# A hybrid encoder layer on one core: a written order with a fixed map of SBUF and PSUM, eight gate tiles moved into block products, and latent attention in quarter tiles

## The chip, the cores and the metric

The kernel runs on one core of a Trainium2 chip. The metric is the device time of one execution in microseconds (us). The core's engines work side by side and meet at semaphores: PE (TensorE, matmuls), DVE (VectorE), ACT (ScalarE), POOL (GpSimd), and SP (SyncE), which here only issues DMAs. PE writes to PSUM, which has eight banks of 128 partitions x 512 float32.

## The reference

One layer on 1024 tokens of 1024 channels, in float32. A single projection of the normed input feeds two attentions and their gates:

```python
h = rmsnorm(x, attn_norm_g)
(c_q, c_kv, k_rope, z_mla, q_dil, k_dil, v_dil, z_dil, g_mla, g_dil) = split(h @ w_in)
a_out = mla_attention(c_q, c_kv, k_rope, ...)       # 8 heads, dense, queries and keys of 64 + 32
y_mla = (a_out * silu(z_mla)) @ w_o_mla
d_out = dilated_mixture(q_dil, k_dil, v_dil, ...)   # 3 groups of 8 heads of 64:
                                                    # (window, dilation) = (128,1), (512,4), (2048,16)
y_dil = (d_out * silu(z_dil)) @ w_o_dil
merged = sigmoid(g_mla + b) * y_mla + sigmoid(g_dil + b) * y_dil
out = rmsnorm(x + merged @ w_out, final_norm_g)
```

The three groups of the dilated mixture are combined by the softmax of their log denominators, so after a pair of heads is done in all three groups, its results are multiplied by factors made from all three.

## The kernel before, in words

Every float32 operand of a product is split into a high part (a cast on ACT, type fp32r) and a low part (a subtraction on DVE or POOL), and a product is three matmuls, high x high, low x high and high x low. That is `mm3` (L77 to L79), and `split` (L83, L84) makes the parts. A **step** below is one such triple with 512 columns.

The work goes in stages. (1) Latents and the values of the dilated groups, up to 221 us. (2) **Block products** up to 452 us: the q and k channels of the dilated groups, in pairs of 128-channel tiles, each pair as a 2 x 2 block matrix product with seven products instead of eight. One product is 4 x 3 = 12 matmuls of 512 columns. Sums of the products on ACT and DVE (`block_steps`, L464), operands and differences on POOL (`block_operand`, `block_minus`), five products ahead. The results go to DRAM (`s_dq`, `s_dk`), and come back in the form that attention wants (`op_b`, `op_a`). (3) **Dilated attention** up to about 800 us: four pairs of heads, three groups in each pair, a unit at a time: scores of two blocks (`s_ps`, L861, L862, and L973 for the widest group), maxima and masks on DVE (L871), exponentials on ACT (L878), transposes on PE (`pt`, L885), their split (ACT L893, DVE L897), values (`av`, L909, L916, L1004), and the result, for which ACT copies one half (`av_t`, L921) and DVE adds the other (`num`, L935). After a pair comes the combine: denominators go through DRAM (`s_sd`, `c_sn`), factors are made from them, go through DRAM too (`s_rr`) and come back spread over partitions (`bc`), where DVE (L1134) and POOL multiply with them. (4) **Latent attention** up to 1142 us: scores of 128 x 1024 (`s_mla`, two banks), maxima (`m_nm`, L741), exponentials (L744), transposes (L755), splits (L83, L84), values (L763, L764). (5) **Output** to the end: what is left of the output projections of both branches (`pj`), the merge with the gates (`gate`, L1183, L1184), and `w_out` with the last norm.

Stages 3 and 4 are pipelines over DVE and ACT in which PE would wait, so PE is given **fillers** between their pieces: first the steps of the 24 tiles of `z` and merge gates (16 steps each; tile results `zg_z`, `zg_t` go to DRAM as `s_zs`, `s_gt`), then the output projections of the dilated branch, then those of the latent branch, as far as they are ready. `feed(n)` gives out n steps on the average; `FIRST_FEED` steps go ahead of the first scores, and `DIL_FEED` and `FEED` are the rates.

What sets the order: in stage 3 the program order is kept on each engine (a manual schedule). In stage 4 and 5 the tile framework's scheduler places instructions, fillers anchored behind a matmul (`issue_after`). Space in SBUF and PSUM is from pools that open and close by stage; a tile that reuses space waits for what used it. In stage 3 the eight banks are two for `pt`, two for `pj`, two tiles of one bank each for `s_ps`, and two of one bank each for `av`. In stage 4 they are two for `pt`, one for `pj`, one for `av`, and two tiles of two banks for `s_mla`. Loads and stores all go through SP's queue in program order, each waiting there for its data.

## Time and profile before

| what | value |
|---|---|
| median of three runs | 1271.56 us (1269.66 to 1273.31) |
| profiled execution, its own time | 1270.74 us |
| span of its trace | 1269.0 us |
| mean granted clock of PE | 0.991 |
| PE busy | 1227.3 us, 97% |
| DVE, ACT, POOL busy | 59%, 48%, 40% |
| chain that ended last: PE, DMA, DVE | 71%, 12%, 5% |
| PE busy, 447 to 473 us (start of dilated attention) | 22.62 of 26 us |
| PE busy, 473 to 800 us (dilated attention) | 317.30 of 327 us |
| PE busy, 800 to 1134 us (latent attention) | 331.42 of 334 us |
| PE busy, 1134 to 1176 us (start of output) | 34.21 of 42 us |
| PE busy, 1176 us to the end | 86.67 of 93 us |

The rows quoted from the trace have a start time, a duration, the engine, the line of the program, the operation, the tiles out<-in, the shape, and in brackets the engine's idle time just before, with what ended it. Starts of matmuls are measured, their ends modelled, so the pace of PE is read from start to start. A row of the waits view names what waited, for what, the total, how often, and the longest. Lines of the kernel before are those of its own listing above; the change has other line numbers.

### The profile page before, as it was taken

To read this page: it belongs to the slowest core of one execution; us is meant where nothing else is said; L and a number is where in the kernel's file an instruction comes from. 1 tells how busy PE (TensorE), PEld (TensorE's weight loads), DVE (VectorE), ACT (ScalarE), POOL (GpSimd) and SP (SyncE) were. 2 spreads that over 40 slices of the span, in tenths; PEclk is the share of its full clock that TensorE was granted. 3 is DMA by queue.
4 is the path that set the end of the run, shared out by engine and by line. 5 is a ranking of instruction groups with operands and counts; after the bars stand their busy time and mean duration, and the time that the engine had idled before them with its cause. 6 is when DMAs were issued, how large, how long until landed. Compare 5 with 4: busy or idle time off the path is not lost.

```text
span 1269.0 us, 19689 instructions
## 1 busy us (share of the span) xinstructions
PE 1227.3 (97%) x6957; PEld 1071.7 (84%) x6957; DVE 750.3 (59%) x1368; ACT 608.1 (48%) x1276; POOL 506.5 (40%) x402
## 2 busy tenths in 40 slices
PE   8999999999999989998999999999999999997998
PEld 8988999788888878887988888888888888885786
DVE  7473525566666645576566664655656666668632
ACT  6633346344434436655555652455555545554422
POOL 2361219887777624526231132312212212237522
PEclk9999999999999999999999999999999999999999
DMA  9957684267456486878889796455336534135441
GB/s 321 273 162 274 220 290 143 92 183 176 125 137 171 128 229 186 212 192 227 210 210 239 185 242 170 152 133 142 113 104 183 134 101 145 59 108 183 165 150 50
DMA packets 134482, 219.43 MB, mean 173 GB/s; under 512 B 37160, under 2 KB 66672, under 8 KB 130480
## 3 DMA queue, kind: packets, MB, share of 16 engines
q1 hardware_dynamic: 134384, 218.17, 59.7%
q8 instruction: 55, 0.90, 0.3%
q14 instruction: 43, 0.35, 0.1%
HBM read 149.37 MB, written 68.75 MB: 172 GB/s over the span
## 4 chain that ended last, share of the span: by engine, by line
PE 71%; DMA 12%; DVE 5%; issue 4%; SPq 3%; POOL 3%; ACT 2%; DVEq 0%; ACTq 0%; POOLq 0%
PE pj L77 12%; PE pj L79 11%; PE pj L78 11%; PE pt L755 4%; SPq L73 3%; PE av L764 2%; PE av L763 2%; DMA bc<-s_rr 2%; PE s_mla L77 2%; PE s_mla L79 2%; PE s_mla L78 2%; PE st_c L77 2%; PE st_c L79 2%; PE st_c L78 2%; PE st_d L77 2%
## 5 line engine op out<-in xcount | busy, mean ns | idle before, releaser
L84 POOL TENSOR_TENSOR w_l<-w_raw,w_h 128x512 fp32r<-128x512 f32 (+1 forms) x176 | 227.6, 1306 | 409.4 <-ACT w_h L83 351.2
L77 PE MATMUL pj<-hT_h,w_h 128*128 128x512 f32 x384 | 157.4, 410 | 0.0
L78 PE MATMUL pj<-hT_l,w_h 128*128 128x512 f32 x384 | 151.7, 395 | 0.0
L79 PE MATMUL pj<-hT_h,w_l 128*128 128x512 f32 x384 | 151.7, 395 | 0.0
L83 ACT CAST w_h<-w_raw 128x512 fp32r<-128x512 f32 (+1 forms) x176 | 104.2, 615 | 89.5 <-POOL w_raw L428 77.6
L84 DVE TENSOR_TENSOR pt_l<-pt,pt_h 128x512 fp32r<-128x512 f32 x128 | 87.9, 688 | 65.7 <-ACT pt_h L83 64.9
L83 ACT CAST pt_h<-pt 128x512 fp32r<-128x512 f32 x128 | 74.5, 584 | 80.8 <-PE pt L755 49.1
L77 PE MATMUL pj<-w_h,hT_h 128*128 128x256 f32 x384 | 109.6, 285 | 0.0
L79 PE MATMUL pj<-w_h,hT_l 128*128 128x256 f32 x384 | 109.5, 285 | 0.0
L78 PE MATMUL pj<-w_l,hT_h 128*128 128x256 f32 x384 | 109.4, 285 | 0.0
L741 DVE TENSOR_REDUCE m_nm<-s_mla 128x1 f32<-128x1024 f32 x64 | 78.1, 1221 | 27.8 <-PE s_mla L79 27.3
L871 DVE CUSTOM_DVE_ANT_0 p<-s_ps,masks 128x256 f32<-128x256 f32 x128 | 48.9, 419 | 66.5 <-PE s_ps L862 57.9
L878 ACT ACTIVATE p<-p,d_st 128x256 f32<-128x256 f32 x128 | 64.1, 502 | 48.3 <-DVE d_st L871 48.0
L79 PEld LDWEIGHTS pj<-hT_h,w_l 128*128 128x128 f32 x384 | 73.0, 190 | 16.3
L77 PEld LDWEIGHTS pj<-hT_h,w_h 128*128 128x128 f32 x384 | 73.6, 192 | 11.1
L78 PEld LDWEIGHTS pj<-hT_l,w_h 128*128 128x128 f32 x384 | 73.7, 192 | 10.9
L744 ACT ACTIVATE p<-s_mla,m_nm 128x1024 f32<-128x1024 f32 x64 | 71.8, 1122 | 17.6 <-PE pt L755 16.8
L755 PE MATMUL pt<-consts,p 128*128 128x128 f32 x512 | 78.0, 272 | 1.6 <-ACT p L744 1.5
L77 PEld LDWEIGHTS pj<-w_h,hT_h 128*128 128x128 f32 x384 | 74.2, 193 | 0.9
L78 PEld LDWEIGHTS pj<-w_l,hT_h 128*128 128x128 f32 x384 | 74.1, 193 | 0.8
L79 PEld LDWEIGHTS pj<-w_h,hT_l 128*128 128x128 f32 x384 | 74.2, 193 | 0.7
L763 PE MATMUL av<-pt_h,op_c 128*128 128x256 f32 x256 | 68.6, 288 | 0.0
(306 smaller groups left out, 3303.3 us busy)
## 6 DMA issues: line engine op xcount, KB each, us to landing
w_raw<-wt SPq DMA_DIRECT2D x48, 512.0 KB, 3.7
op_b<-s_dq SPq DMA_DIRECT2D x32, 512.0 KB, 7.4
gate<-s_gt SPq DMA_DIRECT2D x43, 256.0 KB, 2.9
s_dq<-dq_st SPq DMA_DIRECT2D x80, 128.0 KB, 2.4
s_dk<-dq_st SPq DMA_DIRECT2D x80, 128.0 KB, 2.4
s_dv<-dv_st SPq DMA_DIRECT2D x32, 256.0 KB, 4.6
s_gt<-zg_t SPq DMA_DIRECT2D x32, 256.0 KB, 3.3
w_raw<-wv SPq DMA_DIRECT2D x12, 512.0 KB, 3.8
```

What stands on the lines that cost most here:

```text
L73: self.nc.sync.dma_start(out=out, in_=in_)
L77: mm(out, lh, rh, start=start, stop=False, skip_group_check=skip)
L78: mm(out, lh, rl, start=False, stop=False, skip_group_check=skip)
L79: return mm(out, ll, rh, start=False, stop=stop, skip_group_check=skip)
L83: self.nc.scalar.copy(out=h, in_=raw)
L84: sub.tensor_tensor(out=l, in0=raw, in1=h.bitcast(F32), op=ALU.subtract)
L741: v.tensor_reduce(out=nm[:, hh, qb:qb + 1], in_=s, axis=AX.X, op=ALU.max, negate=True)
L744: nc.scalar.activation(out=p, in_=s, func=AF.Exp, bias=nm[:, hh, qb:qb + 1], accum_out=den[:, hh, qb:qb + 1])
L755: self.anchor = nc.tensor.transpose(pt[:, o:o + 128], P[b2][:, 128 * kc:128 * kc + 128], self.ident)
L763: nc.tensor.matmul(a_out, vv[:, kc], ph[:, s], start=kc == 0, stop=False)
L871: nc.vector.tensor_tensor_reduce(out=p[:, c], in0=x["s"][:, c], in1=mask, op0=ALU.add, op1=ALU.min, scale=-0.125, scalar=3e38, accum_out=s ...
L878: nc.scalar.activation(out=p, in_=p, func=AF.Exp, scale=-1.0, bias=nm, accum_out=den)
```

## The change

Five things change together.

1. **Gate tiles as blocks.** The tiles 8 to 15 (gates of the latent branch), eight of the 24 filler tiles, become four more pairs of block products behind the twelve of q and k. Their sums are multiplied by the row factor (DVE), go through tanh (ACT) and to DRAM (`s_gt`). The fillers of the gate fill fall from 24 to 16 tiles.
2. **One order.** From the end of the block products to the end of the program everything is issued in an order that the program writes out, in a manual schedule.
3. **One map.** SBUF is addressed by fixed offsets in rings (`rings`, `hand`, `get`) from two areas. PSUM has four tiles of one bank (`bank0` to `bank3`) and two tiles of two banks (`bank4`, `bank6`); the rings of `s_ps` and `av2` take the halves of the last two, and `s_mla` the whole of them. In latent attention `pj` keeps one bank, and in the output it takes a ring over the single banks and the halves.
4. **Latent attention in ticks.** A tile of 128 queries x 2 is 4 ticks; in a tick go the transposes of a quarter of the keys, their low, a half of the scores of the next tile, the values of the quarter before, and `feed`. The first ticks overlap the last combine.
5. **Other settings.** Four fillers instead of 19 ahead of the first scores; weights of the output are split earlier, and the last fill steps are kept for the second half of the merge.

```diff
-FIRST_FEED = 19
+FIRST_FEED = 4
 DIL_FEED = (1.43, 1.43, 2.5, 2)
-FEED = (0.95, 0.95)
-NB_S, NB_PT, NB_AV = 2, 2, 1
-ZG = (4, 5, 6, 7, 0, 1, 2, 3, *range(16, 24), *range(8, 16))
+ZG = (4, 5, 6, 7, 0, 1, 2, 3, *range(16, 24))
+BLOCK_GATES = (8, 10, 12, 14)
...
+        self.places.update(pt=b[0:2], pj=b[2:4], s_ps=b[4:6], av2=b[6:8], s_mla=self.wide, m_av=b[3:4])
...
+    def get(self, name, shape=(128, 512), dtype=F32):
+        places = self.places[name]
+        x = places[self.turn[name] % len(places)]
+        self.turn[name] += 1
+        return self.shaped(x, shape, dtype) if isinstance(x, int) else x
...
+                def times():
+                    v.tensor_tensor(out=x, in0=x, in1=self.R[:, c], op=ALU.mult)
+                def tanh():
+                    act.activation(out=t, in_=x, func=AF.Tanh, scale=0.5, bias=self.hb[:, j:j + 1])
+                    self.dma(self.gt[j][:, c], t)
...
+    def mla_tick(self, k, c):
+        self.mla_transposes(k, c)
+        if c == 0:
+            self.mla_low(k, c)
+            self.mla_scores(k + 1, 0)
+            self.mla_values(k - 1, 3)
...
+        elif c == 1:
+            self.mla_exponentials(k + 1, 0)
+            self.mla_low(k, c)
+            self.mla_scores(k + 1, 1)
+            self.mla_values(k, 0)
...
+        else:
+            if c == 2:
+                self.mla_exponentials(k + 1, 1)
+            self.mla_low(k, c)
+            self.feed(self.rate)
+            self.mla_values(k, c - 1)
...
+            if t == 24:
+                run_all(self.fill)
+                self.fill = self.proj_fill()
+                self.owed = 0.0
+            self.rate = 1.8 if t < 24 else 1.55 if t < 112 else 3.0
...
+        self.places["pj"] = [self.banks[i] for i in (2, 4, 5, 6, 7)]
...
+        self.places["pj"] = [self.banks[i] for i in (3, 0, 1, 2, 4, 5, 6, 7)]
...
-                    self.blocks([(T_QK + (g * 2 + quad) * 4 + which * 2, g, quad, which) for quad in range(2) for g in range(3) for which in range(2)], tp, pp)
+                    self.blocks([(T_QK + (g * 2 + quad) * 4 + which * 2, g, quad, which) for quad in range(2) for g in range(3) for which in range(2)] + [(T_ZM + i,) for i in BLOCK_GATES], tp, pp)
+            b = [pp.tile([128, 512], F32, name=f"bank{i}") for i in range(4)]
+            self.wide = [pp.tile([128, S], F32, name=f"bank{i}") for i in (4, 6)]
+            self.banks = b + [x[:, 512 * i:512 * i + 512] for x in self.wide for i in range(2)]
```

How it moves instructions, at three places. First SP's queue at the end of the block products. `s_dq` and `s_dk` are stores of q and k, `op_b` and `op_a` the first loads of attention; in the change `s_gt` are the gate stores, `at5632_2048_r` is the first place of `op_b` and `at22016_1152_r` that of `op_a`. Before:

```order
L73 DMA s_dq2_64<-dq_st10_4651 32x1024 [waits DMAHW3_49,Activation_49]
L73 DMA s_dq2_64<-dq_st10_4651 32x1024 [waits DMAHW4_49]
L73 DMA s_dq2_64<-dq_st10_4651 32x1024 [waits DMAHW5_49]
L73 DMA s_dq2_64<-dq_st10_4651 32x1024 [waits DMAHW6_49]
L73 DMA op_b_4805<-s_dq0_62 64x2048 [waits DMAHW7_49,PE_49]
L73 DMA op_b_4805<-s_dq0_62 64x2048 [waits DMAHW0_49]
L73 DMA op_a_4806<-s_dk0_65 64x1152 [waits DMAHW1_49,PE_49]
L73 DMA op_a_4806<-s_dk0_65 64x1152 [waits DMAHW2_49]
```

and in the change:

```order
L119 DMA s_gt_72<-dq_st00_5363 128x512 [waits DMAHW3_49,Activation_49]
L119 DMA s_gt_72<-dq_st11_5367 128x512 [waits DMAHW4_49,Activation_49]
L119 DMA s_gt_72<-dq_st10_5371 128x512 [waits DMAHW5_49,Activation_49]
L119 DMA s_gt_72<-dq_st01_5376 128x512 [waits DMAHW6_49,Activation_49]
L119 DMA at5632_2048_r_5489<-s_dq0_62 64x2048 [waits DMAHW7_49,Pool_49]
L119 DMA at5632_2048_r_5489<-s_dq0_62 64x2048 [waits DMAHW0_49]
L119 DMA at22016_1152_r_5490<-s_dk0_65 64x1152 [waits DMAHW1_49,Pool_49]
L119 DMA at22016_1152_r_5490<-s_dk0_65 64x1152 [waits DMAHW2_49]
```

The first loads now stand behind four gate stores, each of which waits for an activation of the last gate tiles.

Second, PE in the dilated attention, at a unit of the middle group. Before (`s_ps` and `av2` have a new tile number at each use; `Activation` and `DVE` in the brackets are the counters waited for):

```order
L916 MATMUL av2_5353<-pt_h_5302,op_c_5142 128x256 [waits Activation_49]
L916 MATMUL av2_5353<-pt_l_5303,op_c_5142 128x256 [waits DVE_49]
L916 MATMUL av2_5353<-pt_h_5302,op_c_5142 128x256
L916 MATMUL av2_5353<-pt_l_5303,op_c_5142 128x256
L885 MATMUL pt_5391<-consts_84,p_5310 128x128 [waits PE_49,Activation_49]
L885 MATMUL pt_5391<-consts_84,p_5310 128x128 [waits Activation_49]
L885 MATMUL pt_5391<-consts_84,p_5310 128x128 x2
L861 MATMUL s_ps_5399<-op_a_5160,op_b_5159 128x256
L862 MATMUL s_ps_5399<-op_a_5160,op_b_5159 128x256
```

and in the change, where `bank1` is a `pt`, `bank2` a filler, and every score tile is `bank4_5397` and every value tile `bank6_5398`:

```order
L1056 MATMUL bank1_5394<-consts_84,at97792_512_f_5524 128x128 x2
L1032 MATMUL bank4_5397<-at22016_1152_r_5490,at5632_2048_r_5489 128x256 [waits DVE_49]
L1033 MATMUL bank4_5397<-at22016_1152_r_5490,at5632_2048_r_5489 128x256
L1032 MATMUL bank4_5397<-at22016_1152_r_5490,at5632_2048_r_5489 128x256
L1033 MATMUL bank4_5397<-at22016_1152_r_5490,at5632_2048_r_5489 128x256
L123 MATMUL bank2_5395<-at138752_8192_r_102,w_h_5683 128x512
L124 MATMUL bank2_5395<-at171520_8192_r_103,w_h_5683 128x512
L125 MATMUL bank2_5395<-at138752_8192_r_102,w_l_5684 128x512
L123 MATMUL bank2_5395<-at138752_8192_r_102,w_h_5687 128x512
L124 MATMUL bank2_5395<-at171520_8192_r_103,w_h_5687 128x512
L125 MATMUL bank2_5395<-at138752_8192_r_102,w_l_5688 128x512 [waits Pool_49]
```

Score tiles that alternated between two tiles without a wait of their own now share one tile, and the scores wait for DVE; the same holds for `bank6_5398`, the values.

Third, PE in the latent attention of the change, at a place where one output projection ends and the next begins (`bank2` is the only `pj` bank, `bank3` the values, `bank0` and `bank1` the transposes):

```order
L123 MATMUL bank2_5395<-at122368_1024_r_5429,w_h_9092 128x512
L124 MATMUL bank2_5395<-at134656_1024_r_5430,w_h_9092 128x512
L125 MATMUL bank2_5395<-at122368_1024_r_5429,w_l_9093 128x512
L846 MATMUL bank3_5396<-at60928_512_r_5860,at38400_1024_r_8193 128x256 [waits Activation_49]
L847 MATMUL bank3_5396<-at65024_512_r_5861,at38400_1024_r_8193 128x256 [waits DVE_49]
L846 MATMUL bank3_5396<-at60928_512_r_5860,at38400_1024_r_8193 128x256
L847 MATMUL bank3_5396<-at65024_512_r_5861,at38400_1024_r_8193 128x256
L822 MATMUL bank1_5394<-consts_84,at85504_1024_f_8325 128x128
L822 MATMUL bank1_5394<-consts_84,at89600_1024_f_8344 128x128
L822 MATMUL bank1_5394<-consts_84,at85504_1024_f_8325 128x128
L822 MATMUL bank1_5394<-consts_84,at89600_1024_f_8344 128x128
L123 MATMUL bank2_5395<-at97792_1024_r_5423,w_h_9521 128x512 [waits DVE_49]
```

The first matmul of the new projection waits for DVE to have read the bank, with four values and four transposes between.

More of the change, by code (lines that the diff above doesn't have):

```diff
@@ new lines, in mla_values @@
+    def mla_values(self, k, c):
+        if k < 0:
+            return
+        mm = self.nc.tensor.matmul
+        h, u = self.units[k]
+        if u % 2 == 0 and c == 0:
+            self.av = self.get("m_av")
+        out = self.av[:, 256 * (u % 2):256 * (u % 2) + 256]
+        vv = self.heads[h][2]
+        _, ph, pl = self.pt.pop((k, c))
+        for c2 in range(2):
+            kc = 2 * c + c2
+            x = slice(c2 * 256, c2 * 256 + 256)
+            mm(out, vv[:, kc], ph[:, x], start=kc == 0, stop=False)
+            mm(out, vv[:, kc], pl[:, x], start=False, stop=kc == 7)
@@ new lines, in output, with merge @@
+        mh, ml = {}, {}
+        low = lambda first, n: self.shaped(first, [128, n], F32R)
+        for dt in range(8):
+            mh[dt, 0] = low(49152 + 2048 * dt if dt < 6 else 88064 + 2048 * (dt - 6), 512)
+            ml[dt, 0] = low(32768 + 2048 * dt, 512)
+            mh[dt, 1] = self.hand(RIGHT + 36864 + 4096 * dt, 512, F32R)
+            ml[dt, 1] = low(71680 + 2048 * dt, 512)
+        def merge(dt, half):
+            self.split(self.m1[dt, half], mh[dt, half], ml[dt, half], v)
+        rows = [self.hand(RIGHT + 4096 + 4096 * i, S) for i in range(8)]
@@ new lines, in output @@
+        while self.jobs_done < 24:
+            next(self.fill)
+        for i in range(8):
+            if i < 7:
+                self.wout_load(i + 1, 1)
+            next(self.fill)
+            merge(i, 0)
+            next(self.fill)
+            next(self.fill)
+            self.wout_split(1, nc.gpsimd)
+            while self.jobs_done < 25 + i:
+                next(self.fill)
+        self.dma(gf, a["g_final"].partition_broadcast(128))
+        for t in range(4):
+            first(t)
@@ L1336, in _layout @@
+            self.fill = self.gate_fill()
+            with tc.manual_schedule():
+                self.open_areas()
+                first = len(nc.cur_bb.bb.instructions)
+                self.attention()
+                self.output()
+                self.order_areas(first)
 def _layout(inputs):
```

779 lines of the change are left out of this document (425 added, 354 removed).

## The prediction, made before the changed kernel was run

> **What bounds the kernel now.** I read the page first, then the PE waits stage by stage, then windows and timelines at each wait.
>
> ```profile
> span 1269.0 us, 19689 instructions
> PE 1227.3 (97%) x6957; PEld 1071.7 (84%) x6957; DVE 750.3 (59%) x1368; ACT 608.1 (48%) x1276; POOL 506.5 (40%) x402
> PE 71%; DMA 12%; DVE 5%; issue 4%; SPq 3%; POOL 3%; ACT 2%; DVEq 0%; ACTq 0%; POOLq 0%
> ```
>
> TensorE (PE) is busy for 97%, so its matmuls and its stalls set the time. The waits of PE after the block products, stage by stage (total, times, longest):
>
> ```profile
> PE pt L885 <- ACT p L878: 3.9, 1, 3.9
> PE av L916 <- DVE pt_l L897: 8.4, 5, 3.7
> PE pt L755 <- ACT p L744: 1.5, 1, 1.5
> PE pj L77 <- DVE gate L1183: 4.5, 4, 2.2
> PE pj L77 <- ACT wout_h L83: 2.0, 1, 2.0
> PE pj L77 <- ACT w_h L83: 1.2, 1, 1.2
> ```
>
> Together 21.5 us. After the larger gaps the clock is down: in the windows the column behind POOL is the granted clock.
>
> ```profile
> 473.00:478.00 5.00, 4.48 (x15) 3.70 (x16) 2.92 (x12) 4.64 (x16) 4.50 (x4) 0.50 0.50 157
> 594.00:598.00 4.00, 4.00 (x16) 3.35 (x15) 2.96 (x11) 3.40 (x10) 1.11 (x1) 0.57 0.94 296
> 1161.00:1165.00 4.00, 3.88 (x9) 2.69 (x10) 3.11 (x5) 2.05 (x4) 3.50 (x3) 0.57 0.70 231
> ```
>
> The first costs 5 x 0.50 = 2.5 us, the others 4 x 0.43 = 1.7 us each. The base of the sum is the profiled execution's own 1270.7 us, which is 0.8 us below the median of the runs.
>
> **Fewer matmuls.** Eight gate tiles cost 8 x 2 halves x 8 steps x 3 = 384 matmuls now; as four pairs of block products 4 x 7 x 4 x 3 = 336. All have 512 columns, and these start 0.23 us apart:
>
> ```profile
> 451.46 0.39 PE L77 MATMUL st_d<-hT_h,w_h 128*128 128x512 f32 x1
> 451.69 0.39 PE L78 MATMUL st_d<-hT_l,w_h 128*128 128x512 f32 x1
> ```
>
> 48 x 0.227 = **-10.9 us**, sure from the count. A block pair gives POOL 7 lows and 4 differences of 1.3 us against 7 x 12 x 0.227 = 19 us of PE, so POOL's 14 us stay hidden. The price is elsewhere: steps that fill waits fall from 384 to 256, since the tiles gone were fillers.
>
> ```profile
> L84 POOL TENSOR_TENSOR w_l<-w_raw,w_h 128x512 fp32r<-128x512 f32 (+1 forms) x176 | 227.6, 1306 | 409.4 <-ACT w_h L83 351.2
> ```
>
> **Start of the dilated attention.** Now the loads of the first unit are issued while block products still run (these end at 452.1), and 19 fillers cover the landing:
>
> ```profile
> 446.37 1.14 SPq L73 DMA_DIRECT2D op_b<-s_dq  x2
> 447.60 1.18 SPq L73 DMA_DIRECT2D op_a<-s_dk  x2
> DMA to landing us min/median/max: 8.4/11.6/14.8
> 469.24 0.39 PE L79 MATMUL pj<-hT_h,w_l 128*128 128x512 f32 x1
> 473.52 0.97 PE L885 MATMUL pt<-consts,p 128*128 128x128 f32 x3 [3.89 <-ACT p L878]
> ```
>
> From the first issue to the last landing of the four are about 10.2 us (the second op_a is issued at 448.2 and takes 8.4). In the change four gate stores stand ahead of them on SP, and the last can't go before add, product (DVE) and tanh (ACT) of the last tile:
>
> ```profile
> L84 DVE TENSOR_TENSOR pt_l<-pt,pt_h 128x512 fp32r<-128x512 f32 x128 | 87.9, 688 | 65.7 <-ACT pt_h L83 64.9
> 516.72 0.63 ACT L620 ACTIVATE zg_t<-zg_z 128x512 f32<-128x512 f32 x1 [0.25 <-DVE zg_z L618]
> ```
>
> 2 x 0.69 + 0.63 = 2.0 us after the last product; landing is 12.2 us after it; four fillers are 4 x 0.68 = 2.7 us. PE idles 9.5 us and then pays the slow clock (2.5), 12.0 against today's 3.9 + 2.5 = 6.4: **+5.6 us**. If with less traffic the loads take 8 us it is +3.4; if they are as slow as the median of 11.6, +8.8.
>
> **Shared halves: steady units.** Today a score tile and a value tile have a bank each, two in turn. In the change both live as halves of one two-bank tile, and PE's rows wait for a DVE counter at every reuse of either half: the values of a unit wait until DVE has taken the result of the unit just before, and scores wait for the maxima just before. Whether today's result would be late is seen by laying the two timelines side by side:
>
> ```profile
> 516.56 0.28 PE L916 MATMUL av<-pt_h,op_c 128*128 128x256 f32 x1
> 516.60 1.09 DVE L935 TENSOR_TENSOR num<-av,av_t 64x512 f32<-64x512 f32 x1
> 532.28 0.28 PE L916 MATMUL av<-pt_h,op_c 128*128 128x256 f32 x1
> 532.40 1.09 DVE L935 TENSOR_TENSOR num<-av,av_t 64x512 f32<-64x512 f32 x1
> ```
>
> The result ends at 517.69 where the next values start at 516.56, and at 533.49 where they start at 532.28: late by 1.1 and 1.2 us. Laid out over the whole stage, 13 of the 40 value tiles are late in this way outside the combines, by 0.1 to 1.9 us, 12.5 us in all; the tiles of the first, narrow group never are. PE is in order, and what follows on DVE waits for PE's next scores, so a wait is not made up later. I take **+12.5 us**; low 4 (DVE comes to the result sooner because it is less behind after each wait), high 16.
>
> **Shared halves: combines.** After each pair DVE multiplies by factors that come back by DMA, and stands in its queue until they land:
>
> ```profile
> DVE num L1134 <- DMA bc<-s_rr: 27.3, 12, 5.3
> 580.84 0.69 DVE L1134 TENSOR_TENSOR num<-num,bc 128x512 f32<-128x512 f32 x1 [5.28 <-DMA bc<-s_rr]
> 590.59 1.44 DVE L1134 TENSOR_TENSOR num<-num,bc 128x512 f32<-128x512 f32 x1 [2.74 <-DMA bc<-s_rr]
> 582.36 0.28 PE L916 MATMUL av<-pt_h,op_c 128*128 128x256 f32 x1
> 583.76 0.39 PE L916 MATMUL av<-pt_l,op_c 128*128 128x256 f32 x1 [1.12 <-DVE pt_l L897]
> 590.61 0.28 PE L916 MATMUL av<-pt_h,op_c 128*128 128x256 f32 x1
> 593.38 0.39 PE L916 MATMUL av<-pt_l,op_c 128*128 128x256 f32 x1 [2.49 <-DVE pt_l L897]
> DVE num L1134 <- DMA bc<-s_rr: 4.0, 3, 2.6
> ```
>
> DVE stands 27.3 us, PE only 8.4: PE runs a score tile, fillers and a value tile ahead. The maxima and results queued behind that wait are what PE now asks for one tile sooner. The last row is the last pair alone, 4.0 us (with pieces at the window's edge 5); of the other 22, in seven waits, a slack of about one filler and a half (1 us) remains each: 15 us of stall, against 8.4, and two results late besides (3 us): **+9.5 us**. The low end is 0, if the factors land earlier; the high end 22 - 8.4 + three slow clocks of 1.7 = +19.
>
> **Latent attention.** A pair's tile now takes four ticks. The merge projections that fill it use one PSUM bank, as before, but two steps are given out together, so that a job's end and the next job's start can stand a few matmuls apart, with the DVE read of the bank between. On DVE the low of a split is ahead, and that waits for ACT's cast:
>
> ```profile
> L83 ACT CAST pt_h<-pt 128x512 fp32r<-128x512 f32 x128 | 74.5, 584 | 80.8 <-PE pt L755 49.1
> L675 DVE SCALAR_TENSOR_TENSOR m<-gate,pj 128x512 f32<-128x512 f32 x16 | 10.9, 679 | 4.6 <-PE pj L79 4.6
> 583.98 0.28 PE L916 MATMUL av<-pt_h,op_c 128*128 128x256 f32 x1
> 584.10 0.28 PE L916 MATMUL av<-pt_l,op_c 128*128 128x256 f32 x1
> 584.22 0.60 PE L885 MATMUL pt<-consts,p 128*128 128x128 f32 x4
> 584.57 0.37 PE L861 MATMUL s_ps<-op_a,op_b 128*128 128x256 f32 x1
> ```
>
> 0.58 + 0.69 + 0.68 = 1.95 us on DVE's side, against four values (0.48) and four transposes (0.35) on PE's: 1.1 us each. The order has ten such places (where values and transposes don't stand between, more): **+10 us** with about 1 us each, 4 to 15. Besides, the gate fill ends in the fourth of 32 tiles and the next fill begins three tiles later, and the last combine, covered today by fillers, runs into these ticks: its 5 us, and a little for bare tiles, **+5.5 us** (0 to 12).
>
> **Output.** The six-row list above has 7.7 us of waits here, and 1.7 of slow clock; eleven fill steps kept for this place and the weights split earlier remove most. But the ring of banks contains both halves of the same two tiles, so a part waits for DVE and ACT to leave the neighbour: 4 x 1.4 us (0.69 and 0.63 again). 5.6 - 9.4 = **-4 us** (-9 to +5).
>
> Sum: -10.9 + 5.6 + 12.5 + 9.5 + 10 + 5.5 - 4 = +28.2, so **1299 us**. The low ends give -10.9 + 3.4 + 4 + 0 + 4 + 0 - 9 = -8.5 (1262), the high ends +65 (1336); they won't all fall on one side, and 1278 to 1322 is the likeliest case's own range.
>
> **Beside the trace.** The Trainium skill (PSUM — Partial Sum Buffer, "Summary: rules for kernel authors") lets a matmul run while another engine reads a different bank, so that the chip itself asks for no wait between two halves. By that rule 12.5 and 9.5 drop out, and the sum is 1277; the waits in the rows of the change say otherwise, and no run here shows it yet. The Trainium skill (TensorE: Matmul & The Clock Gate, "What's actually happening") has the clock fall after an idle window of about 3.4 us; the trace has 0.57 in 594 to 598, right behind the gap of 2.49 us that ends at 593.38, so that the shorter stalls can cost clock as well, and the measurement decides.
>
> **Rivals.** (a) The fixed order absorbs the waits: faster. The mechanism is slack in DVE's order: DVE is 59% busy, and if results and maxima are done one filler sooner than in today's trace (1.2 us), no steady unit waits. Then the combines cost no more than now, the start and latent attention about +5 together, and the output gives its 9.4: 1270.7 - 10.9 + 5 - 9.4 = 1255; with the existing stalls of 8.4 gone too, 1247. For it: lateness is small, never above 1.9 us. Against: DVE's order of maxima, low and result in a unit is the old one. It decides where the mean lateness falls below 0.3 us. (b) The waits hold per half, not per tile: 1277. Against it stand the rows quoted ahead. (c) Gains and stalls cancel: half of the steady waits and of the job waits, the combines as now: 1299 - 6 - 9.5 - 5 - 5.5 = 1273. (d) The stalls feed on each other: six more gaps of 2.5 us or more with 1.7 us of slow clock each, and bare tiles at the high end (6 more): 1316 and above, to 1335.
>
> **Chances.** Forecast 0.52, (a) 0.22, (b) 0.10, (c) 0.08, (d) 0.08. Within 0.3% is 1267.8 to 1275.4, about the least that a measurement of this kernel tells from no change; (c) gives most of "same" and the forecast, (b) and (d) are slower: faster 0.24, same 0.07, slower 0.69. To leave out no more than 2 in 10, the range reaches down into (a): 1245 to 1322.
>
> **What would show it.** Right: in the waits of PE, scores and values waiting for maxima and results some dozens of times at about 1 us; a PE gap of 8 to 11 us behind the block products; a merge projection waiting for its own DVE read ten times. Wrong: value tiles that start before the result ahead of them has ended; first loads issued before the last gate store; a stretch of the output as long as now. Most of all the forecast falls if the shared halves cost less than 6 us in the dilated stage.

## The result, and the profile after

The changed kernel takes **1358.38 us** (1357.66 to 1362.83, four runs) against 1272.43 of the kernel before in the same series (1269.66 to 1273.70, four runs): a ratio of 1.069, with a 95% interval of 1.066 to 1.072. The forecast was 1299 us with a range of 1245 to 1322. The direction was right, and the size was not: +86 us instead of +28.

The page of the changed kernel, first the span, then the engines' busy time and the chain that ended last:

```profile
span 1356.7 us, 19579 instructions
PE 1243.8 (92%) x6909; PEld 1077.3 (79%) x6909; DVE 745.6 (55%) x1360; ACT 625.7 (46%) x1304; POOL 554.7 (41%) x448
PE 65%; DMA 10%; DVE 10%; POOL 5%; ACT 4%; issue 4%; SPq 2%; ACTq 0%; DVEq 0%; POOLq 0%
```

PE has the 48 matmuls less that were counted (6957 to 6909). Yet it is idle for 1356.7 - 1243.8 = 112.9 us, against 41.7 before (+71.2), and it is busy for 16.5 us more with 10.9 us of matmuls less, so that its matmuls took 27.4 us longer: the granted clock fell from 0.991 to 0.969, and busy time x (1 - clock) gives 38.6 us against 11.0, nearly the same difference. The whole is 71.2 + 27.4 - 10.9 = 87.7 us of span. Busy time is thus no measure here of work done: the slow clock is counted in it.

Where it goes is seen in windows that hold the same stages in both kernels (the columns are as in the prediction: length, PE, its loads, DVE, ACT, POOL, granted clock, DMA share, GB/s). The kernel before, from the end of the block products: start of dilated attention, the rest of it, latent attention, start of the output, its rest.

```profile
447.00:473.00 26.00, 22.62 (x104) 18.52 (x102) 11.16 (x20) 6.34 (x14) 4.15 (x6) 0.97 0.94 238
473.00:800.00 327.00, 317.30 (x1899) 280.19 (x1900) 198.53 (x507) 174.90 (x446) 117.64 (x104) 0.98 0.80 207
800.00:1134.00 334.00, 331.42 (x1925) 285.89 (x1924) 207.69 (x273) 180.27 (x327) 70.98 (x57) 1.00 0.43 124
1134.00:1176.00 42.00, 34.21 (x148) 25.56 (x147) 33.69 (x41) 17.13 (x30) 28.28 (x20) 0.96 0.51 165
1176.00:1269.00 93.00, 86.67 (x405) 72.56 (x404) 40.26 (x84) 27.72 (x63) 31.08 (x23) 0.99 0.34 121
```

The changed kernel, the same five stages:

```profile
524.00:548.00 24.00, 13.53 (x54) 11.05 (x53) 5.87 (x16) 5.39 (x13) 3.41 (x8) 0.72 0.80 203
548.00:890.00 342.00, 305.89 (x1812) 265.38 (x1811) 194.69 (x480) 169.65 (x430) 108.87 (x96) 0.96 0.72 188
890.00:1215.00 325.00, 290.54 (x1689) 249.94 (x1689) 206.21 (x280) 174.71 (x316) 69.03 (x54) 0.95 0.39 110
1215.00:1260.00 45.00, 38.13 (x149) 29.11 (x148) 18.81 (x23) 15.21 (x28) 41.08 (x31) 0.92 0.49 164
1260.00:1357.00 97.00, 84.22 (x389) 69.22 (x388) 33.77 (x73) 24.00 (x58) 23.48 (x18) 0.99 0.23 81
```

The idle time of a row is its length less PE's busy time, and its slow clock costs busy time x (1 - clock); the clock has two digits, so a sum over the stages is good to some 5 us. Lost in this way:

| stage | before, idle + slow clock | after, idle + slow clock | difference | forecast |
|---|---|---|---|---|
| dilated attention with its start | 13.1 + 7.0 | 46.6 + 16.0 | +42.5 | +27.6 |
| latent attention | 2.6 + 0 | 34.5 + 14.5 | +46.4 | +15.5 |
| output | 14.1 + 2.2 | 19.7 + 3.9 | +7.2 | -4 |

The waits of PE in the changed kernel, to be held against those in the prediction (total, times, longest). First the dilated attention in three windows; `L1032` are scores, `L1087` and `L1175` values, `L1106` and `L1181` the results on DVE, `L1042` the maxima:

```profile
PE bank L1032 <- DMA at_r<-s_dk: 10.5, 1, 10.5
PE bank L1087 <- DVE at_f L1106: 1.9, 3, 1.1
PE bank L1175 <- DVE at_f L1181: 0.4, 1, 0.4
...
PE bank L1087 <- DVE at_f L1106: 11.2, 4, 6.3
PE bank L1032 <- DVE at_f L1042: 2.8, 3, 1.8
PE bank L1175 <- DVE at_f L1181: 0.4, 1, 0.4
...
PE bank L1087 <- DVE at_f L1106: 13.1, 6, 5.8
PE bank L1032 <- DVE at_f L1042: 2.2, 1, 2.2
PE bank L1175 <- DVE at_f L1181: 0.9, 1, 0.9
```

Then from 860 to 1240 us, in two windows. `L762` is the read of the fillers' bank by a job of the dilated branch, `L764` the same of the latent branch, `L691` that of a gate tile; `L846` and `L847` are values, `L824` a cast, `L830` a low, and `L880` the transposes of a half's factors:

```profile
PE bank L847 <- DVE at_r L830: 5.3, 5, 3.4
PE bank L846 <- ACT at_r L824: 4.7, 3, 1.9
PE bank L880 <- DVE m_d L878: 4.1, 2, 2.2
PE bank L123 <- DVE zt L691: 2.1, 1, 2.1
...
PE bank L123 <- DVE at_f L762: 7.8, 8, 1.4
PE bank L123 <- DVE zt L764: 6.8, 6, 1.4
PE bank L880 <- DVE m_d L878: 3.7, 4, 1.7
```

And from 1240 us to the end:

```profile
PE bank L123 <- ACT bank L1418: 6.2, 4, 1.5
PE bank L123 <- DVE zt L764: 3.0, 1, 3.0
```

The longest waits of the dilated attention stand in the combines. At one of them, in the timelines of PE and then of DVE:

```profile
673.06 1.23 PE L1087 MATMUL bank<-at_r,at_r 128*128 128x256 f32 x4 [6.32 <-DVE at_f L1106]
```

```profile
665.80 0.69 DVE L1341 TENSOR_TENSOR at_f<-at_f,at_f 128x512 f32<-128x512 f32 x1 [1.00 <-DMA at_f<-s_rr]
671.96 1.05 DVE L1106 TENSOR_TENSOR at_f<-bank,at_f 64x512 f32<-64x512 f32 x1 [3.58 <-DMA s_da<-at_f]
```

After DVE had its factors (`s_rr`) it stood once more, for 3.58 us, since the result of the next unit goes to a place from which a finished result was still being stored to DRAM (`s_da`). The values of the unit after it, whose half lies in the same tile, waited for that result: 6.32 us on PE. In the 4 us behind it the granted clock is 0.60:

```profile
673.00:677.00 4.00, 3.94 (x17) 3.71 (x18) 0.98 (x6) 1.77 (x4) 0.58 (x1) 0.60 0.14 54
```

### The profile page after: what moved, and what is told of

Read it like the earlier page. It is cut to its first block, busy times and chain, and to the rows that moved or that the text cites. A ratio compares the mean times of both kernels' runs of the same rounds, so it can differ in the third digit from the quotient of the medians.

```text
span 1356.7 us, 19579 instructions
## 1 busy us (share of the span) xinstructions
PE 1243.8 (92%) x6909; PEld 1077.3 (79%) x6909; DVE 745.6 (55%) x1360; ACT 625.7 (46%) x1304; POOL 554.7 (41%) x448
## 4 chain that ended last, share of the span: by engine, by line
PE 65%; DMA 10%; DVE 10%; POOL 5%; ACT 4%; issue 4%; SPq 2%; ACTq 0%; DVEq 0%; POOLq 0%
PE bank L123 8%; PE bank L125 7%; PE bank L124 7%; PE bank L822 3%; PE st_a L123 2%; PE st_a L125 2%; PE st_a L124 2%; PE st_d L123 2%; PE st_c L123 2%; PE st_d L124 2%; PE st_c L124 2%; PE st_d L125 2%; PE st_c L125 2%; PE pj L123 2%; PE pj L124 2%
## 5 line engine op out<-in xcount | busy, mean ns | idle before, releaser
L130 POOL TENSOR_TENSOR w_l<-w_raw,w_h 128x512 fp32r<-128x512 f32 x192 | 249.1, 1312 | 319.9 <-ACT w_h L129 265.1
L123 PE MATMUL bank<-at_r,w_h 128*128 128x512 f32 x384 | 162.6, 423 | 20.5 <-DVE zt L764 9.8
L129 ACT CAST w_h<-w_raw 128x512 fp32r<-128x512 f32 x192 | 114.8, 622 | 106.0 <-POOL w_raw L474 94.9
L125 PE MATMUL bank<-at_r,w_l 128*128 128x512 f32 x384 | 154.3, 402 | 1.3 <-POOL w_l L130 1.3
L124 PE MATMUL bank<-at_r,w_h 128*128 128x512 f32 x384 | 154.4, 402 | 0.0
L830 DVE TENSOR_TENSOR at_r<-bank,at_r 128x512 fp32r<-128x512 f32 x128 | 88.3, 690 | 104.0 <-ACT at_r L824 103.8
L824 ACT CAST at_r<-bank 128x512 fp32r<-128x512 f32 x128 | 74.9, 586 | 89.8 <-PE bank L822 89.2
L123 PE MATMUL bank<-at_r 96*128 96x512 f32 (+2 forms) x264 | 109.1, 413 | 6.9 <-ACT bank L1418 6.2
L123 PE MATMUL pj<-w_h,at_r 128*128 128x256 f32 x384 | 108.9, 284 | 0.0
L124 PE MATMUL pj<-w_l,at_r 128*128 128x256 f32 x384 | 108.8, 283 | 0.0
L125 PE MATMUL pj<-w_h,at_r 128*128 128x256 f32 x384 | 108.7, 283 | 0.0
L123 PEld LDWEIGHTS bank<-at_r,w_h 128*128 128x128 f32 x384 | 75.0, 195 | 38.2 <-DVE at_f L762 11.8
L125 PE MATMUL bank<-at_r 96*128 96x512 f32 (+2 forms) x264 | 103.6, 393 | 0.0
L124 PE MATMUL bank<-at_r 96*128 96x512 f32 (+2 forms) x264 | 103.1, 391 | 0.0
L1042 DVE CUSTOM_DVE_ANT_0 at_f<-bank,masks 128x256 f32<-128x256 f32 x128 | 49.0, 420 | 97.8 <-PE bank L1033 97.6
L806 DVE TENSOR_REDUCE m_nm<-bank 128x1 f32<-128x1024 f32 x64 | 78.1, 1220 | 10.9 <-PE bank L125 8.6
L474 POOL TENSOR_TENSOR w_raw<-w_raw 128x512 f32<-128x512 f32 x64 | 83.7, 1308 | 0.0
L124 PEld LDWEIGHTS bank<-at_r,w_h 128*128 128x128 f32 x384 | 75.2, 196 | 10.5
```

Source lines behind the costliest of these rows:

```text
L123: mm(out, lh, rh, start=start, stop=False, skip_group_check=skip)
L124: mm(out, lh, rl, start=False, stop=False, skip_group_check=skip)
L125: return mm(out, ll, rh, start=False, stop=stop, skip_group_check=skip)
L129: self.nc.scalar.copy(out=h, in_=raw)
L130: sub.tensor_tensor(out=l, in0=raw, in1=h.bitcast(F32), op=ALU.subtract)
L474: self.nc.gpsimd.tensor_tensor(out=b[out], in0=b[x], in1=b[y], op=ALU.subtract)
```

## The experiments

Eighteen kernels were run. All changed the program's order, its places, the form of the gate tiles or the engine of a sum, and none left out a part of the computation. Times with a ratio are medians of two to twelve runs, the ratio with its 95% interval; the others are single runs, good to about half a per cent (the twelve runs of `lows_ahead` go from 1257.75 to 1273.62 us), so that a difference of 6 us or less between two of them shows little. The kernel before, run beside them, had medians of 1267.3 to 1272.1 us.

**The shared halves.** `own_banks` gives scores and values of the dilated attention four tiles of one bank again, and makes the two wide tiles of them only when latent attention begins:

```diff
+                op = self.own[n].enter_context(tc.tile_pool(name=f"own{n}", ..., bufs=1, space=PSUM, side=side))
+                self.banks += [op.tile([128, 512], F32, name=f"bank{4 + 2 * n + i}") for i in range(2)]
-            self.wide = [pp.tile([128, S], F32, name=f"bank{i}") for i in (4, 6)]
-            self.banks = b + [x[:, 512 * i:512 * i + 512] for x in self.wide for i in range(2)]
...
+                self.widen(1)
...
+                self.widen(0)
```

> The change, with one edit: in the dilated stage the two score tiles and the two value tiles are four tiles of one bank each again, which become two wide tiles only when latent attention begins. Theory (shared halves): of the 49 us of PE stalls and 16 us of slow clock between 528 and 885 us, the waits for the results (L1106, L1181) and the maxima (L1042), 37 us, fall to the 10 us that the kernel before had there, and the slow clock to about 7: 1358 - 27 - 9 = 1322 us, and in the combines DVE still stands for its DMAs while PE does not. Rival (the DMAs of a combine, the factors and the store of the pair's result that frees its tile, are simply late in the new order): only the steady 11 us go, the four stalls of 3.6 to 6.5 us stay: 1345. Rival (too few fillers): nothing changes, 1356.

1332.96 us (ratio to the kernel before 1.050, 1.045 to 1.056): 25.4 us less than the change, and 11 us short of its theory. The waits for results and maxima are gone. What is left of the dilated attention's waits behind the start has other names (`L1076` is a low, `L1057` the exponentials):

```profile
PE bank L1095 <- DVE at_r L1076: 6.6, 6, 2.3
...
PE bank L1064 <- ACT at_f L1057: 3.8, 3, 1.8
```

`before_halves` does the opposite: the kernel before, with these four tiles alone put together as halves.

```diff
-                s = x["s"] = self.sp.tile([128, 512], F32, name="s_ps", bufs=NB_S)
+                s = x["s"] = self.half("s_ps", self.sp)
...
-                    av = o["av"] = self.avp.tile([128, 512], F32, name="av2", bufs=2)
+                    av = o["av"] = self.half("av2", self.avp)
```

> The kernel before with one thing of the change: the two score tiles of the dilated stage are halves of one two-bank tile, and so are the two value tiles; everything else as before, with its 19 and 24 tiles of fillers. Theory (the shared halves alone cost what separate banks gave back in the change, 25 us with thin filling and 36 with dense): 1272 + 30 = 1302 us, with waits of the values for the results. Rival (they hurt only together with the new order): under 1280.

1294.79 us against 1267.55: +27. In its waits from 450 to 810 us the results (`L944`) stand first; the second row is the wait at the start of the stage, which was 3.9 us before:

```profile
PE av L925 <- DVE num L944: 24.7, 15, 4.9
PE s_ps L870 <- DVE d_st L880: 5.8, 1, 5.8
```

This is decisive, since nothing else differs: with the old scheduler in stages 4 and 5, the old fillers and the old order of stage 3, the halves cost 27 us. The two kernels without gate blocks, `gates_back` (24 filler tiles, higher rates) and `gates_back_own` (the same and own banks), ask whether more fillers would hide it:

```diff
-DIL_FEED = (1.43, 1.43, 2.5, 2)
+DIL_FEED = (2.3, 2.3, 3.4, 2.9)
-ZG = (4, 5, 6, 7, 0, 1, 2, 3, *range(16, 24))
-BLOCK_GATES = (8, 10, 12, 14)
+ZG = (4, 5, 6, 7, 0, 1, 2, 3, *range(16, 24), *range(8, 16))
+BLOCK_GATES = ()
```

> The change with its first part undone: tiles 8 to 15 are fillers again (24 tiles, no gate blocks), and the rates in the dilated stage are raised from 1.43, 1.43, 2.5, 2 to 2.3, 2.3, 3.4, 2.9, so that the fillers end at the same place as in the change. Theory (fillers are what hides the waits; 48 more matmuls, 10.9 us, come back): of the 49 us of stalls and 16 us of slow clock in the dilated stage more than half go: 1358 + 11 - 38 = 1331 us. Rival (the shared halves cost the same whatever the filling): 1358 + 11 - 5 = 1364.

> The same with a bank of its own for each score and value tile in the dilated stage. Theory (fillers and separate banks buy the same cover, so that the second adds little): the dilated stage as in the kernel before, and 1322 us, 10 less than with the filling alone. Rival (the two are independent): 1333 + 11 - 30 = 1314. In both, what is left over the 1272 of the kernel before sits in latent attention and output, and is then due to the ticks and not to the dilated stage.

1368.57 and 1332.22 us, the second 10 us above its theory. Fillers don't hide it: the halves cost 36 us with dense fillers, no less than with sparse ones. In `gates_back_own`, PE has no wait in the dilated attention but the one at its start, a single row from 450 to 810 us:

```profile
PE bank L1040 <- DMA at_r<-s_dk: 17.2, 1, 17.2
```

So DVE is fast enough for this stage, and the waits were those of the shared tile. The one row also says something of the start: it is longer than the 10.5 us of the change although no gate store stands ahead of the loads. The last eight stores of k (`s_dk`) stand there in the written order, and the loads go out at 461.5 us; in the kernel before they went out at 446.4, ahead of those stores. So what costs is to stand behind the stores of the last block, whichever these are.

**The gate blocks.** `gates_back` is 10.2 us slower than the change. That this is so near to the 10.9 us of the 48 matmuls is in part luck: its start waits 7 us longer (17.5 us instead of 10.5), and other waits of the dilated attention are shorter. With own banks the blocks gain nothing (1332.22 without, 1332.96 with): what they save is lost again in the rows of `own_banks` above, waits for lows and exponentials that `gates_back_own`, with more steps to fill with, doesn't have. `before_gates` puts the blocks alone into the kernel before:

```diff
-ZG = (4, 5, 6, 7, 0, 1, 2, 3, *range(16, 24), *range(8, 16))
+ZG = (4, 5, 6, 7, 0, 1, 2, 3, *range(16, 24))
+BLOCK_GATES = (8, 10, 12, 14)
```

> The kernel before, with the first part of the change alone: the tiles 8 to 15 are four pairs of block products, and the fillers fall from 24 tiles to 16; order, pools, ticks and settings as before. Theory: 48 matmuls less are 10.9 us, and what the missing fillers cost is small, since latent attention has slack on DVE and ACT: 1272 - 10.9 + 5 = 1266 us. Rival (the missing fillers are the main part of the 87 us): 1300 or more.

1324.61 us, a ratio of 1.044 (1.037 to 1.050), where a gain was expected. The gate fill runs dry before the last pair is combined, and the next fill can't begin before the pieces of the dilated branch (`brd_h`) are ready. PE then stands for 26 us at a stretch; later it waits for lows in latent attention, which the missing fillers covered. The waits from 520 to 900 us, then from 900 us on:

```profile
PE pj L78 <- ACT brd_h L84: 27.9, 2, 26.0
...
PE av L785 <- DVE pt_l L85: 13.6, 16, 4.2
PE pj L78 <- DVE gate L1204: 11.8, 6, 3.8
```

The changed kernel, with its fill moved by hand, doesn't have the first of these. So the block form of the eight gate tiles is 10.9 us cheaper, by the count, and their worth as cover was larger.

**The start.** `first_feed_20` gives out 20 fillers ahead of the first scores instead of 4.

```diff
-FIRST_FEED = 4
+FIRST_FEED = 20
```

> The change with 20 fillers instead of 4 ahead of the first scores. Theory (the loads stand behind the gate stores, and four fillers are too few): the gap of 10.6 us and the 2.5 us of slow clock behind it go, at the cost of 16 fillers (10.9 us) that are missing in the first ticks of latent attention, where PE has other work between: 1358 - 10 = 1348 us. Rival (fillers are what is scarce, so that each one moved only moves the hole): 1358.

1371.88 us, slower by 13.5. The gap didn't go, it got another cause. The weights of the third filler tile were asked for, and on ACT their cast now stands ahead of the first exponentials and waits for their load, while PE waits for the exponentials. ACT's timeline and PE's longest wait at the start:

```profile
553.11 1.14 ACT L129 CAST w_h<-w_raw 128x512 fp32r<-128x512 f32 x2 [13.70 <-DMA w_raw<-wt]
554.16 0.51 ACT L1049 ACTIVATE at_f<-at_f,at_f 128x256 f32<-128x256 f32 x1
```

```profile
PE bank L1056 <- ACT at_f L1049: 9.7, 1, 9.7
```

**Latent attention and output.** `job_gap` lets no `feed` end one job and begin the next:

```diff
+            done = self.jobs_done
...
+            if self.jobs_done > done:
+                break
```

> The change, except that a feed never starts a projection in the same feed in which another ended; the steps left over are given out later. Theory (one bank, DVE's read between two jobs): of the 17 us of waits of L123 for L762, L764 and L691 from 885 to 1215 us some 10 go, 1348 us. Rival (the steps put off only come back as bare time in the output): 1357.

1353.38 us: 5.0 less, half of what was expected and not clear of the noise of a single run; from 960 to 1215 us ten waits at boundaries are left:

```profile
PE bank L126 <- DVE zt L767: 3.3, 3, 2.5
PE bank L126 <- DVE at_f L765: 3.2, 7, 0.8
```

So a job that ends as a group of fillers ends still waits, when little stands between it and the next. 

`mend` puts four things to `own_banks`: `job_gap`, the transposes of the factors a tick after their making, the split of a piece of the dilated branch a tick later, and a ring for the output in which the halves of a tile don't follow each other.

```diff
-        self.places["pj"] = [self.banks[i] for i in (3, 0, 1, 2, 4, 5, 6, 7)]
+        self.places["pj"] = [self.banks[i] for i in (3, 4, 0, 6, 1, 5, 2, 7)]
...
+            self.mla_factors_out(k)
...
-                self.split(y, self.brd[0][j][:, x], self.brd[1][j][:, x], nc.gpsimd)
+                late[t + 1] = j, x, y
```

> The change with five mends: separate banks in the dilated stage; no feed ends one projection and starts the next; a piece of the dilated branch is split one tick after its product; the transpose of the factors of a half goes into the next tick; in the output neighbours in the ring of banks come from different tiles. Theory (the named waits are the loss): from 1333, 9 for L880, 7 for the casts behind a piece, 5 for the jobs, 7 for L1418: 1305 us. Rival (a wait taken away at one place comes back at the next, since DVE and ACT set the pace where fillers are missing): 1322 or more.

1306.71 us, 26 less than `own_banks`, as its theory had it. The waits for `L1418` are gone, those for the factors fell to one of 1.1 us. `mend_14` adds 14 fillers ahead, and `mend_14_late` uses each piece three ticks after its load instead of two, and lets the read of a gate tile follow its last matmul at once:

> The five mends and 14 fillers instead of 4 ahead of the first scores. Theory (the gap of 10.6 us is filled, 20 was slower because the twentieth filler puts a cast of weights, whose load comes late, ahead of the first exponentials): 9 us less than with the five mends, 1296. Rival (fillers moved only move the hole): no difference.

> The five mends with 14 fillers, and two waits of DVE's order moved: a piece of the dilated branch is used three ticks after its load instead of two, and a gate tile's product that reads the only filler bank stands right behind its last matmul. Theory (the first tiles of latent attention lose 29 us because DVE stands for loads in front of the lows): 1300 - 8 = 1292 us, the combine's part stays. Rival (with no fillers there PE waits for the next thing instead): 1300.

1300.54 and 1293.54 us. 14 fillers gain 6 us, hardly clear of the noise, where 20 lost 13.5. In `mend_14` PE's waits from 840 to 945 us are mostly for lows of the first, bare tiles; DVE itself stands there for loads of the gated pieces:

```profile
PE bank L858 <- DVE at_r L841: 11.1, 6, 5.0
```

```profile
DVE zt L1000 <- DMA at_f<-s_zs: 8.6, 3, 4.4
```

`mend_14_late` came out at its theory's 1292, but not in its theory's way. In the same window PE waits for lows as long as before, and DVE still stands 11.3 us for those loads:

```profile
PE bank L861 <- DVE at_r L844: 14.4, 10, 4.3
```

What is better is the granted clock, 0.93 instead of 0.84 from 870 to 945 us. Why is open, and 7 us between two single runs is little.

**The order without halves and blocks.** `spread_0` has all mends, 24 filler tiles and no gate blocks; `spread_2` has two gate blocks, `spread_4` four.

```diff
-ZG = (4, 5, 6, 7, 0, 1, 2, 3, *range(16, 24))
-BLOCK_GATES = (8, 10, 12, 14)
+ZG = (4, 5, 6, 7, 0, 1, 2, 3, *range(16, 24), 8, 9, 10, 11, 12, 13, 14, 15)
+BLOCK_GATES = ()
...
-            self.rate = 1.8 if t < 24 else 1.55 if t < 112 else 3.0
+            self.rate = 4.0 if t < 24 else 1.55 if t < 112 else 3.0
```

> The change with the five mends (no job or gate tile begins in the feed in which another ends), no gate blocks, 16 fillers ahead of the first scores, and rates of 2.0, 2.0, 3.1, 2.6 in the dilated stage, so that 43 fill steps are left for the first six tiles of latent attention (rate 4 there). Theory (latent attention loses where the last combine runs through ticks that have no fillers): from 1332, 26 for the mends, 16 for the start, 18 for those tiles: 1272 us. Rival (the ticks themselves are slower than the old tiles, fillers or not): 1290.

> The same with two of the four gate blocks, rates 1.6, 1.6, 2.6, 2.2, 16 fillers ahead and 42 steps left for the first six tiles. Theory: 24 matmuls, 5.4 us, less than with no blocks, and the dilated stage still covered: 1268 us, the least of the three. Rival: between the two others.

> The mends with all four gate blocks and 14 fillers ahead, the rates of the dilated stage lowered to 1.2, 1.2, 2.1, 1.8, so that 43 steps are left for the first six tiles. Theory: the stalls between 852 and 935 us (24, and 7 of slow clock) go for the most part, those of the dilated stage (14) grow by some 10: 1300 - 12 = 1288 us. Rival (fillers are worth the same everywhere): 1300.

1299.93, 1317.76 and 1321.28 us, with ratios of 1.025 (1.018 to 1.032), 1.039 (1.032 to 1.047) and 1.042 (1.034 to 1.051). All three were missed by 28 to 50 us. One reason is that fillers that run through the first tiles of latent attention need the only bank, and its read by a gate tile (`L702`) was issued only with the next half. That is 13.9 us in `spread_0`, 10.8 and 14.7 in the others, and so not the whole of it. In `spread_0` from 440 to 860 us, and from 860 to 1130:

```profile
PE bank L134 <- DVE zt L702: 7.7, 2, 5.6
...
PE bank L134 <- DVE zt L702: 6.2, 3, 2.1
```

`combine_first` keeps that, and runs the last combine over ten groups of fillers ahead of the ticks; `spread_0_late` instead lets the read follow at once, and has the later pieces of `mend_14_late`.

```diff
+        for t in range(first, first + 10):
+            self.feed(2.2)
+            for f in later.pop(t, []):
+                f()
+            self.feed(2.2)
```

> From the kernel with mends, no gate blocks and 43 fill steps kept (1300 us): the last combine runs to its end over those fillers, with two filler banks, before the ticks begin, as in the kernel before; the pieces of the dilated branch follow ten ticks earlier. Theory (the overlap of the last combine with the ticks is what costs in the first tiles): of 26 us of stalls and 8 of slow clock from 835 to 980 us two thirds go, 1300 - 22 = 1278 us. Rival (ticks without fillers lose as much in their own waits): 1295 or more.

> The kernel with mends, no gate blocks and 43 fill steps kept, with a gate tile's product right behind its last matmul and the pieces one tick later. Theory (15 us of waits for L702 come only from the product standing behind a tick's other work): 1300 - 13 = 1287 us. Rival (one bank for the fillers costs that wherever the product stands): 1297.

1286.51 us (ratio 1.015, 1.011 to 1.019), between its theory and its rival, and 1279.76, 7 less than its theory. The read of the bank together with the later pieces was worth 20 us, the place of the combine 13; no run has the read alone. Three kernels on the base of `spread_0_late` then move a few instructions each. `loads_ahead` issues the first loads on POOL's queue, ahead of the last stores; `loads_ahead_dve` has in addition the sums of the merge on DVE in the output; `lows_ahead` in addition two lows of weights ahead of POOL's release of the last area.

```diff
+                if i == 7:
+                    self.queue = nc.gpsimd
+                    between()
+                    self.queue = nc.sync
+                    self.weights_split(1)
...
-                nc.gpsimd.tensor_tensor(out=m1, in0=t, in1=m1, op=ALU.add)
+                (v if len(self.places["pj"]) > 1 else nc.gpsimd).tensor_tensor(out=m1, in0=t, in1=m1, op=ALU.add)
```

> The best order so far (spread_0_late, 1279.8), with the four loads of the first two heads' queries and keys issued on GpSimd's queue right behind the release of their space, instead of on SyncE behind the last block's stores. Theory (the start gap is only the place of these loads in SyncE's queue): the loads go out at about 448 instead of 460, land at about 458, and the 16 fillers last until about 460, so the gap of 9.7 us and its 1.9 us of slow clock go: 1268 (1266 to 1272). Rival (the loads are late because of the memory traffic of the last stores, or of the results that attention itself waits for): the gap keeps 5 us or more, 1275 and above.

> The same as loads_ahead, and in the output the sum of the two merged halves of each job on VectorE instead of GpSimd. Theory (in the output TensorE waits for GpSimd's lows of weights because this sum, 1.3 to 1.7 us each, stands between them; 6.7 us of waits): 6 us less than loads_ahead, 1262 (1259 to 1266), below the kernel before. Rival (the lows are late because of the loads of the weights and of the casts ahead of them): no difference to loads_ahead, 1268.

> loads_ahead_dve (1272.7) with one more move on GpSimd: the two lows of the second filler tile's weights stand ahead of the operation that waits until the last block's stores have landed (the release of the last area), not behind it. Theory (that release took the place of the loads: TensorE waited 7.9 us for these lows, since the operation ahead of them stood 15 us for the stores): the fillers run on, about 2 us remain at the start because the first exponentials need the same area, and some 6 us go: 1267 (1263 to 1270). Rival (whatever is moved, the start waits for the landing of the last stores, since the first maxima and exponentials need the area too): 1272.

1281.57 us (ratio 1.009, 1.006 to 1.011), 1272.70 (1.002, 1.000 to 1.005) and 1266.82 (0.998, 0.996 to 1.001). `loads_ahead` was a miss: the loads went out at 451 us instead of 460 and landed in time, but another wait took their place. POOL's release of the last area waits for the last stores to land (`s_dk`), and behind it on POOL stood the lows of the next filler. POOL's timeline, and PE's wait:

```profile
451.01 1.26 POOL L132 DMA_DIRECT2D at_r<-s_dq  x2
470.28 0.09 POOL L1226 MEMSET left<- 1x1 f32 x1 [14.98 <-DMA s_dk<-dq_st]
471.16 2.51 POOL L143 TENSOR_TENSOR w_l<-w_raw,w_h 128x512 fp32r<-128x512 f32 x2
```

```profile
PE bank L138 <- POOL w_l L143: 7.2, 1, 7.2
```

With the lows ahead of it, as expected, 2.3 us are left, which wait for the exponentials that need the same area:

```profile
PE bank L1086 <- ACT at_f L1079: 2.3, 1, 2.3
```

In the output the sum on DVE did what its theory said: waits for lows of weights fell from 5.8 us to 0.6. `lows_ahead` can't be told from the kernel before, and it has neither the halves nor the blocks: no variant was shown to beat the kernel before.

## Why the prediction was right or wrong

The direction was right. Of the forecast's terms, those for latent attention (+15.5, measured +46.4), for the combines and for the output were wrong in size, the last in sign too, and slow clock was missing in the sum.

- **Fewer matmuls, -10.9:** right, from the count of 6909. The 10.2 us that `gates_back` gives back are no proof, as said above.
- **Start, +5.6:** the mechanism and nearly the size were right. The wait was 10.5 us (9.5 forecast), its slow clock 13.53 x 0.28 = 3.8 (2.5); 14.3 against 6.4 before is +7.9. The loads stood behind the stores, as forecast: the first left at 530.86 us, 2.9 us behind the last product (2.0 forecast), and the scores began 10.5 us after that (10.2). But the gate stores aren't what matters, as `gates_back_own` shows.
- **Steady units, +12.5:** the mechanism was right, the size a little high. Of the 20 waits for results and maxima in the rows above (32.9 us in all), nine lie in the combines (between DVE's wait for the denominators and its result behind the last store). The other 11 make 7.5 us, between the forecast's own 4 and 16.
- **Combines, +9.5:** this step failed, in its size and in what DVE stands for. The nine waits are 25.4 us, where 15 + 3 were forecast; five of them (6.3, 5.8, 4.3, 3.5 and 2.2 us) make 22.1. The step took "seven waits with a slack of about one filler and a half" from the waits for factors alone. These are only 11.2 us on DVE from 640 to 885 us, where the forecast had 22. It left out that DVE, behind the factors, also waits for the stores of finished results, 9.3 us in three places (from 640 to 750, and from 750 to 885 us):

```profile
DVE at_f L1106 <- DMA s_da<-at_f: 3.6, 1, 3.6
...
DVE at_f L1106 <- DMA s_da<-at_f: 5.7, 2, 3.4
```

Each of the three stands right ahead of one of the three longest waits of PE (6.32, 4.33 and 5.75 us). In `gates_back_own` DVE has them too (5.34, 3.26 and 6.46 us), and PE waits for none of them: it is the shared tile that hands them on. The store isn't needed for the loss, though: in `before_halves` DVE has no such wait, and the halves cost 27 us. Together with the steady units, 32.9 against the 8.4 before is +24.5 where the two terms gave +22. Beyond that came slow clock, which the step counted only in the high end: 12 us behind the start, where the kernel before has not above 7. The halves as a whole, forecast +22, cost 25 (`own_banks`), 27 (`before_halves`) and 36 (`gates_back`).
- **Latent attention, +10 and +5.5:** this step failed most, with +46.4. "Ten places with about 1 us each" became 15 waits at boundaries with 16.7 us in the rows above (two of the six for `L764`, 2.5 us, lie in the output already). Three things weren't seen in the order at all: transposes of factors placed directly behind DVE's making of them (7.8 us), values behind casts and lows that are late in the tiles without fillers (10.0 us, forecast 5.5 together with the combine), and, behind the stalls, 14.5 us of slow clock where the kernel before has none that two digits show. `mend`, with the same bank and the same ticks, took 26 us of that and of the output (53.6 together) back, so that about half of it was places in queues; how the 26 divide among its four parts no run shows. `lows_ahead` keeps the ticks and the single bank as well and is level with the kernel before, so the ticks themselves needn't cost.
- **Output, -4:** wrong in sign, +7.2. The 4 x 1.4 for the halves were right (6.2 us in four waits). But the 9.4 that should have gone were replaced: merge jobs wait for DVE's read of the job before (5.5 us in three waits, the longest 3.0 us), and DVE stands there for the load of a gate that was asked for one job ahead (10.2 us in five waits from 1215 to 1260 us); others wait for POOL's lows, 1.3 us. `loads_ahead_dve`, where 5.2 us of such waits went, shows that the latter were a matter of the place in POOL's queue. That the gate's load is what DVE waits for is read from the trace, and no run moved it.
- **Rivals.** (b), waits per half, has fallen: `before_halves` shows a wait per tile. The Trainium skill's rule that a matmul may run while another engine reads a different bank (PSUM — Partial Sum Buffer, "Summary: rules for kernel authors") would have given 1277; it doesn't decide here, since the program itself asks for a wait. (a) and (c) fell too. (d), "the stalls feed on each other", was nearest: 27.4 us of slow clock, of which the forecast's sum had none as new; it stood at 0.08 and to 1335 only, since its other half, new waits in latent attention, was not in it.
- **What the forecast lacked in method.** I walked the new order of PE at places I already suspected, and priced each wait by one duration. In an order that is fixed on all engines each wait is the last of a chain of queues; a walk through DVE's and ACT's new order in the first eight tiles of latent attention would have shown transposes and casts that follow their producer at once.

Open is what the store of finished results would be worth with the halves kept: no run took that wait away alone.

## What to carry to other kernels

Put two tiles that are used in turn into one wide tile only where nothing waits on either: semaphores follow the tile, and 22 us of such waits counted in the old trace became 25 to 36. Price work that fills by what it covers too: eight tiles made cheaper by 10.9 us cost the old order, which leaned on them, 56 us in all. And when a wait is moved, look for what is next in the same queue: at the start it went from DMA to ACT in one variant, and from DMA to POOL to ACT in another, before it was down to 2.3 us.

## What had not been expected of the hardware

The clock is a term of its own. No work was added, and matmuls took 27.4 us longer, as the granted clock is low behind stalls (0.60 in the 4 us after the gap of 6.32 us, 0.72 in the window of the start). This kernel, with several dozen stalls more, paid about 0.4 us of slow clock for each us more that PE stood: 27.4 against 71.2. How the stalls lie seems to matter. From 890 to 960 us PE stands for 13.3 of 70 us, at a clock of 0.85, which is 8.5 us; from 960 to 1215 us it stands for 21.2 of 255 us, mostly in waits of about 1 us, at 0.98, which is some 5 us.

And more cover can be slower: 20 fillers ahead instead of 4 cost 13.5 us, since they bring a cast of weights ahead of the first exponentials on ACT, which stood there for 13.7 us until the load had landed.
